# A two-layer decoder step on one core: low parts of the first output weights on VectorE, another projection order for two head pairs, and other ranks and slacks for the woven work

## The chip, the core and the metric

The kernel runs on one core of one Trainium2 chip. The metric is the device time of one execution in microseconds (us). In the profile the engines are PE (TensorE; PEld is its weight load), DVE (VectorE), ACT (ScalarE), POOL (GpSimd) and SP (SyncE, whose queue issues nearly all DMAs here).

## The reference

One inference step of a decoder with two layers, on a prompt of 1024 tokens and on 8 samples of 4 tokens (32 rows). Each layer computes `x + gate · Branch(RMSNorm(x)(1 + scale) + shift)`, with shift, scale and gate from a condition vector. The first branch is attention with a window of 128, 16 query heads and 4 key/value heads of 64. The second is gated DeltaNet with 16 value heads of 128, here taken as 8 pairs of heads that share a key head, in chunks of tokens. Cut to what matters:

```python
def swa_branch(h, w_in, sinks, w_out, k_buf=None, v_buf=None):
    q, k, v, z = jnp.split(h @ w_in, [...], axis=-1)
    attn = swa_prompt_core(q, k, v, sinks)            # samples: cached keys and values before them
    out = (attn * jax.nn.silu(z)) @ w_out

def gdn_branch(h, conv_buf, s0, w_in, conv_w, ...):
    xqkv, z, a, b = jnp.split(h @ w_in, [...], axis=-1)
    q, k, v = jnp.split(silu(conv(xqkv)), [...], axis=-1)   # q, k normalized
    # per chunk: a triangular system is solved (w_v, w_k), then in turn
    u = w_v_c - w_k_c @ S
    o = q_dec_c @ S + qk_c @ u
    S = S * g_tot_c + k_dec_c.T @ u
    out = (rms_norm(o, o_norm_g) * silu(z)) @ w_out
```

Outputs are both groups' final rows, the new key and value caches, the new convolution tails and the new DeltaNet states (8 samples × 16 heads × 128 × 128 and the prompt's). Everything is float32.

## The kernel before

**Products.** A large product is made as three TensorE products of split operands. Each operand is held as a high part (a rounded copy, made on ACT, as in `wh<-wr`) and a low part (raw minus high, a subtraction on DVE or POOL, as in `wl<-wr,wh`), and the products are high·high, high·low and low·high. The small products of the recurrence stay fp32. So TensorE's stream changes often between split products of 288, 384 or 512 columns and short fp32 products.

**Stages in time.** Attention runs to about 360 us (its opening, to about 70 us, is written out by hand), the samples' attention over cached keys from 360 to 388, the first layer's output projection from 394 to about 520, the eight DeltaNet pairs from 520 to 1353, and the closing from there: the second output projection, the samples' states and the final norm.

**What sets the order.** From the end of the opening on, the program's order is set by a planner inside the kernel. The stream of projection products is the backbone (`project`). Everything else is a job, a generator that yields a condition, issues some instructions and yields the next. `weave(gen, name, hq)` puts a job into the list by rank: `KT[name]` in the closing, `KR[hq][name]` for the jobs of one head pair, `K[name]` otherwise; a smaller rank comes first. After every projection product `stages()` goes through the list in that order and lets each job run as long as its condition holds. A condition can count products or columns passed (`later`, `pos[0] >= ...`), or compare times of a cost model that `Core.issued` keeps for each engine: `ready` wants the operands finished at TensorE's present time, `sure(by, ...)` with a margin, `soon` and `idle` with a slack (`AM`, and `AT` in the closing, in tenths of a us). The engines then run their streams in the order issued, and wait where an operand is late.

**Names and lines that follow.** L318 `SP` holds how many ticks after a projection's start its successor's two halves of weights are split (`ahead` in `projected`, L656 to L672). L1425 `load_wo` loads the first layer's output weights in sixteen pieces of 128x512 through four buffers, with three loads under way, each piece through

```python
                nc.scalar.copy(hi, raw)
                eng = "gpsimd" if hf else "vector"
                yield idle(eng, hi)
                getattr(nc, eng).tensor_sub(lo, raw, f(hi))
                placed.add((j, hf))
                fetch()
```

`ORD` (L2384) holds the order of the projections q, z, k and v of each pair; k belongs to the next pair. `chain` is the recurrence of a pair, eight steps in sequence: `S,kT` (TensorE), `vo` (DVE), `vo,UZ` (TensorE, into `ps_ob`), `uo` (ACT), `uo,ks` (TensorE), the new `S` (DVE); `S,qT` and `uo,DP` are the step's outputs. `vT`, `zl`, `Xd` and `UZ` are operands that ACT, DVE and POOL make for the pairs (`vT` and `zl` are turned on TensorE afterwards, into `ps_tr`). `modG,selt` spreads the gate rows over the partitions for the closing. `olo` and `ohi` are parts of the gated heads for the second output projection, `S1w` the samples' new states.

Of the kernel before, what the change touches and what calls it, by code (L numbers as in the profile page):

```python
# [18 lines left out]
NB = TP // P  # L19
# [278 lines left out]
def body(tc, I, O, cst_ap, dbg=None):  # L298
# [16 lines left out]

    nkeep = COFF["wmask"][0]
    ZB, VB, SB = 2, 3, 6
    SP = (1, 20)  # L318
    AM = (3, 12)
    AT = (-5, 5)  # L320
    EX = (2.2, 2.5, 0.8, 0.7)
    ES, EN, EL, EM = EX
    K = {'split': 13, 'add': 6, 'attend': 26, 'turning': 2, 'modulate': 27, 'cached': 16, 'wo': 48, 'turn': 0, 'ahead': 2, 'taps': 2, 'gating': 5, 'decay': 24, 'samples': 38, 'load': 6, 'mod': 1, 'shape': 9, 'decays': 23, 'prepare': 0, 'gather': 17, 'finish': 32, 'states': 28, 'core': 33, 'new': 11}
    KT = {'prepare': 3, 'gather': 35, 'finish': 63, 'states': 10, 'core': 7, 'new': 18, 'load': 27, 'gating': 6, 'samples': 6, 'output': 20}
    KR = [{'chain': 1, 'output': 3, 'solve': 5, 'invert': 21, 'blocks': 35, 'decayed': 22}, {'chain': 30, 'output': 2, 'solve': 19, 'invert': 31, 'blocks': 39, 'decayed': 37}, {'chain': 9, 'output': 2, 'solve': 29, 'invert': 19, 'blocks': 5, 'decayed': 11}, {'chain': 23, 'output': 23, 'solve': 4, 'invert': 4, 'blocks': 7, 'decayed': 17}, {'chain': 13, 'output': 11, 'solve': 12, 'invert': 7, 'blocks': 29, 'decayed': 27}, {'chain': 9, 'output': 15, 'solve': 6, 'invert': 16, 'blocks': 49, 'decayed': 27}, {'chain': 0, 'output': 1, 'solve': 11, 'invert': 20, 'blocks': 29, 'decayed': 14}, {'chain': 10, 'output': 2, 'solve': 33, 'invert': 28, 'blocks': 1, 'decayed': 53}]
    TB = (3, 0)
    SW = (20, 7)
    MS = (34, 13)
    AH, AI = (a / 10 for a in AM)
    ORD = ['zzkv', 'zqzvk', 'qzzkv', 'qzzvk', 'qzzkv', 'qvzzk', 'qzzkv', 'qvzz']  # L330
    MM = (8, 12)
    ORDER = [("q", 2), ("q", 3), ("q", 4), ("q", 5), ("z", 0), ("k", 1), ("z", 1), ("z", 2), ("q", 6), ("q", 7),
             ("z", 3), ("z", 4), ("z", 5), ("z", 6), ("z", 7)]
    SE = ("vector", "vector", "vector", "vector")
# [675 lines left out]
    if True:  # L1010
# [414 lines left out]
        def load_wo(j0):  # L1425

            pieces = [(j, hf) for j in range(j0, j0 + 4) for hf in range(2)]
            raws_ = []
            if j0:
                yield over("ahead")  # L1430

            def fetch():
                if pieces:
                    j, hf = pieces.pop(0)
                    pr, g = j // 4, j % 4
                    raw = (wp.tile([P, 512], F32, tag="wr", name="wr", bufs=4) if j0 else
                           sa.tile([P, 512], F32, tag="wor", name="wor", bufs=4))
                    for a in range(2):
                        hd = (2 * pr + a) * 4 + g
                        nc.sync.dma_start(raw[64 * a:64 * a + 64], wo_rows[hd * 64:hd * 64 + 64, hf * 512:(hf + 1) * 512])  # L1440
                    raws_.append((j, hf, raw))

            for _ in range(3):
                fetch()
            while raws_:
                j, hf, raw = raws_.pop(0)
                cs = slice(hf * 512, (hf + 1) * 512)
                hi, lo = whi[j][:, cs], wlo[j][:, cs]
                yield idle("scalar", raw)
                nc.scalar.copy(hi, raw)  # L1450
                eng = "gpsimd" if hf else "vector"
                yield idle(eng, hi)
                getattr(nc, eng).tensor_sub(lo, raw, f(hi))
                placed.add((j, hf))
                fetch()
# [5 lines left out]
        load, step, end = modulation_gate(0, at, 8, "wg")  # L1461
# [86 lines left out]
    if True:  # L1548
# [24 lines left out]
        def add_out(pj, i, t, hf):  # L1573

            parts = P if t < NB else TS
            ns = slice(hf * 512, (hf + 1) * 512)
            yield lambda: gathered[0] == 2 * i + hf and i in rows_
            xt = rows_[i][0:parts]
            if t < NB:
                yield idle("vector", pj)  # L1580
                y = x2.tile([P, 512], F32, tag="y", name="y", bufs=2)
                nc.vector.tensor_tensor(y, pj, gate[:, ns], ALU.mult)
                opened.pop(0)
            else:
# [12 lines left out]
                give("lg", pg)  # L1597
            eng = "vector" if i == NB and hf else "gpsimd"
            yield idle(eng, y, xt)
            getattr(nc, eng).tensor_tensor(xt[:, ns], xt[:, ns], y[0:parts], ALU.add)  # L1600
            if hf == 0:
                rows_["ss", i] = sm.tile([P, 2], F32, tag="ss", name="ss")[0:parts]
            yield soon(xt)
            nc.scalar.activation(y[0:parts], xt[:, ns], AF.Square, accum_out=rows_["ss", i][:, hf:hf + 1])
            gathered[0] += 1
            if hf == 1:
                nc.sync.dma_start(x1d[t * P:t * P + parts], xt)
                weave(shape(i, t, xt, rows_["ss", i], parts), "shape")
                if t == NB:
                    weave(modulation_gate(1, wp, 4, "wr"), "mod")  # L1610
# [272 lines left out]
    if True:  # L1883
# [446 lines left out]
        def load_out(*cuts):  # L2330
# [14 lines left out]
            while raws_:  # L2345
                hf, k, ns, raw = raws_.pop(0)
                yield lambda: whs[k] is not None
                yield sure(EL, raw)
                hi, lo = whs[k][:, ns], wls[k][:, ns]
                yield idle("scalar", raw)  # L2350
                nc.scalar.copy(hi, raw)
                eng = "gpsimd" if k % 2 else "vector"
                yield idle(eng, hi)
                getattr(nc, eng).tensor_sub(lo, raw, f(hi))
                loaded.add((k, hf))
                fetch()
# [60 lines left out]
        def prepare(b, part, t):  # L2417
# [5 lines left out]
            for kk in range(2):  # L2423
# [16 lines left out]
                olo = x3.tile([P, 4, P], F32R, tag="olo", name="olo", bufs=2)  # L2440
                yield idle("scalar", of)
                nc.scalar.copy(ohi, of)
                eng = "gpsimd" if kk else "vector"
                yield idle(eng, ohi)
                getattr(nc, eng).tensor_sub(olo, of, f(ohi))
                ohl.append((ohi, olo))
# [47 lines left out]
        def gather(pj, n, part, t, hf):  # L2494
# [541 lines left out]
```

## Time and profile before

| | |
|---|---|
| runs | 1619.73, 1619.86, 1620.67 us; median 1619.86 |
| profiled execution | 1618.79 us, span 1617.0 us |
| mean granted clock of TensorE | 0.997 |
| TensorE busy | 1581.2 us of the span |
| VectorE, ScalarE, GpSimd busy | 1204.8, 843.0, 222.7 us |
| DMA | 195.7 MB, mean 121 GB/s |

The three runs differ by 0.94 us. The profile is one further execution; its time lies 1.07 us under the median, and its span leaves out 1.8 us around the program. A busy TensorE is a modelled figure, since matmuls overlap: what it loses is better read from the starts of neighbouring products, and from the rows of waits, which give for a group of products the total idle time ahead of them, how often, and the longest.

### The profile page before, as it was taken

What the parts mean: (1) busy time and instruction counts of PE and PEld (TensorE: products, weight loads), DVE (VectorE), ACT (ScalarE), POOL (GpSimd) and SP (SyncE); (2) the same over time, 40 slices, a digit from 0 to 9 for tenths busy, and PEclk for the clock granted to TensorE, in tenths of its full rate; (3) what the DMA queues carried; (4) which work ended last, traced back from release to release, by engine and by line L of the source; (5) the groups of instructions that cost most, each with busy time, mean ns of one, the idle gap of its engine ahead of it and who ended that gap; (6) DMA issues with size and microseconds to landing.
All of it is one profiled execution on the core that took longest, in us unless ns stands there. A gap on an engine that the chain in (4) does not pass through costs nothing.

```text
span 1617.0 us, 30791 instructions
## 1 busy us (share of the span) xinstructions
PE 1581.2 (98%) x10714; PEld 1403.0 (87%) x10714; DVE 1204.8 (75%) x3773; ACT 843.0 (52%) x2422; POOL 222.7 (14%) x292
## 2 busy tenths in 40 slices
PE   9999999999999999999999999999999999999997
PEld 6888888988678999989999999998999997757776
DVE  5737677565665678987988769897679877858776
ACT  4635555444344655576465655665456564523332
POOL 1300000002223002020020000202002013233332
PEclk9999999999999999999999999999999999999999
DMA  9442220116343333233423324414243146685874
GB/s 363 154 140 79 79 81 28 40 51 148 105 146 108 106 84 80 81 90 80 133 53 95 99 57 113 99 49 120 61 126 76 45 104 195 207 270 169 298 264 165
DMA packets 178828, 195.72 MB, mean 121 GB/s; under 512 B 76848, under 2 KB 120720, under 8 KB 178640
## 3 DMA queue, kind: packets, MB, share of 16 engines
q1 hardware_dynamic: 178672, 193.75, 40.2%
q8 instruction: 85, 1.39, 0.4%
q14 instruction: 71, 0.58, 0.1%
HBM read 146.45 MB, written 49.27 MB: 121 GB/s over the span
## 4 chain that ended last, share of the span: by engine, by line
PE 77%; DVE 7%; DMA 5%; issue 4%; ACT 4%; POOL 2%; SPq 1%; POOLq 0%; DVEq 0%; ACTq 0%
PE ps_pj L84 45%; PE ps_mi L84 12%; PE ps_lg L84 9%; PE ps_ob L84 5%; PE ps_tr L84 4%; DMA zo<-in_xT 1%; ACT jc L84 1%; PE ps_pj L1480 1%; POOL xt L84 1%; SPq L84 1%; DVE vT L84 1%; DMA out_new_s_s<-S 1%; DVE hlo L84 1%; DVE fu L84 1%; PE ps_tr L1480 1%
## 5 line engine op out<-in xcount | busy, mean ns | idle before, releaser
L84 PE MATMUL ps_pj<-h2lo,wh 128*128 128x384 f32 (+1 forms) x1128 | 377.4, 335 | 0.0
L84 PE MATMUL ps_pj<-h2hi,wh 128*128 128x384 f32 (+1 forms) x1128 | 377.4, 335 | 0.0
L84 PE MATMUL ps_pj<-h2hi,wl 128*128 128x384 f32 (+1 forms) x1128 | 375.8, 333 | 1.2 <-DVE wl L84 1.2
L84 PEld LDWEIGHTS ps_pj<-h2hi,wl 128*128 128x128 f32 x1128 | 212.7, 189 | 3.7 <-DVE wl L84 1.5
L84 PEld LDWEIGHTS ps_pj<-h2lo,wh 128*128 128x128 f32 x1128 | 212.9, 189 | 2.3
L84 PEld LDWEIGHTS ps_pj<-h2hi,wh 128*128 128x128 f32 x1128 | 212.7, 189 | 2.3
L84 POOL TENSOR_TENSOR Xd<-Xc,cst 32x128 f32<-32x128 f32 x128 | 67.0, 524 | 436.8 <-DMA Xc<-Xdd 347.7
L84 PE MATMUL ps_pj<-hhi,wh 128*128 128x384 f32 (+1 forms) x376 | 123.9, 332 | 0.5 <-ACT hhi L84 0.4
L84 PE MATMUL ps_pj<-hlo,wh 128*128 128x384 f32 (+1 forms) x376 | 123.5, 331 | 0.1
L84 PE MATMUL ps_pj<-hhi,wl 128*128 128x384 f32 (+1 forms) x376 | 122.1, 328 | 0.0
L84 DVE TENSOR_TENSOR wl<-wr,wh 128x512 fp32r<-128x512 f32 x120 | 84.2, 703 | 19.4 <-ACT wh L84 18.6
L84 DVE SCALAR_TENSOR_TENSOR vT<-XR,cT,vT 128x384 f32<-128x384 f32 (+1 forms) x144 | 83.5, 588 | 11.8 <-ACT vT L84 10.5
L84 POOL TENSOR_TENSOR xt<-xt,y 128x512 f32<-128x512 f32 (+1 forms) x47 | 65.7, 1400 | 164.7 <-DVE y L84 137.6
L84 ACT CAST wh<-wr 128x512 fp32r<-128x512 f32 x128 | 78.5, 615 | 14.3 <-PE ps_pj L84 13.4
L84 PEld LDWEIGHTS ps_pj<-hlo,wh 128*128 128x128 f32 x376 | 70.6, 188 | 10.6 <-issue 9.8
L84 PEld LDWEIGHTS ps_pj<-hhi,wh 128*128 128x128 f32 x376 | 70.5, 188 | 6.7 <-issue 4.6
L84 ACT COPY XR<-ps_pj 128x384 f32<-128x384 f32 (+1 forms) x96 | 43.3, 451 | 60.1 <-PE ps_pj L84 60.0
L84 PEld LDWEIGHTS ps_pj<-hhi,wl 128*128 128x128 f32 x376 | 70.6, 188 | 3.7 <-issue 3.7
L84 ACT ACTIVATE qe<-ps_mi,Eg 128x128 f32<-128x128 f32 x112 | 35.0, 363 | 67.5 <-PE ps_mi L84 61.1
L84 DVE TENSOR_TENSOR X<-X,tmp 128x126 f32<-128x126 f32 (+22 forms) x248 | 63.8, 257 | 8.5
L84 ACT ACTIVATE prob<-prob,nm 128x256 f32<-128x256 f32 (+1 forms) x128 | 62.4, 491 | 14.1 <-DVE nm L84 13.8
L84 DVE TENSOR_TENSOR tmp<-X 128x126 f32<-128x126 f32 (+22 forms) x248 | 62.4, 252 | 6.2 <-POOL X L84 1.9
(557 smaller groups left out, 3866.1 us busy)
## 6 DMA issues: line engine op xcount, KB each, us to landing
wr<-in_gwb SPq DMA_DIRECT2D x96, 256.0 KB
S<-in_states SPq DMA_DIRECT2D x42, 256.0 KB
wm<-in_wm SPq DMA_DIRECT2D x16, 512.0 KB
wr<-in_winb SPq DMA_DIRECT2D x32, 256.0 KB
wmod<-in_w_mod SPq DMA_DIRECT2D x32, 256.0 KB
wm<-in_w_mod SPq DMA_DIRECT2D x32, 256.0 KB
DP<-gcr SPq DMA_DIRECT2D x64, 128.0 KB
zl<-zd SPq DMA_DIRECT2D x32, 256.0 KB
```

Of the source, the lines that this page charges most:

```text
L84: inst = fn(*args, **kwargs)
L1480: mm = nc.tensor.matmul(pv, x[:, k, t * P:t * P + parts], y[:, k % 2, :], start=(n == 0), stop=(n == 23))
```

## The change

The low parts of the first layer's output weights are all made on DVE (`GP[0]` is 0; eight subtractions of 128x512 leave POOL). The other entries of `GP` are 1 and leave their lines as they were. Pair 2 projects in the order z, q, z, k, v instead of q, z, z, k, v, and pair 5 in the order v, q, z, z, k instead of q, v, z, z, k. All ranks are drawn anew, most of them with other values. The split of the next weights may start after two ticks instead of one (`SP`), the slack of `idle` in the closing is 0.3 us instead of 0.5 (`AT`), the margin for the samples' states 1.7 us instead of 2.2 (`EX`), and three schedules by position have other starts and strides (`SW`, `MS`, `MM`).

```diff
-    SP = (1, 20)
+    SP = (2, 20)
     AM = (3, 12)
-    AT = (-5, 5)
-    EX = (2.2, 2.5, 0.8, 0.7)
+    AT = (-5, 3)
+    EX = (1.7, 2.5, 0.8, 0.7)
...
-    KT = {'prepare': 3, 'gather': 35, 'finish': 63, 'states': 10, 'core': 7, 'new': 18, 'load': 27, 'gating': 6, 'samples': 6, 'output': 20}
+    KT = {'prepare': 3, 'gather': 33, 'finish': 24, 'states': 19, 'core': 7, 'new': 14, 'load': 19, 'gating': 6, 'samples': 5, 'output': 23}
...
-    SW = (20, 7)
-    MS = (34, 13)
+    SW = (35, 1)
+    MS = (39, 13)
     AH, AI = (a / 10 for a in AM)
-    ORD = ['zzkv', 'zqzvk', 'qzzkv', 'qzzvk', 'qzzkv', 'qvzzk', 'qzzkv', 'qvzz']
-    MM = (8, 12)
+    GP = (0, 1, 1, 1, 1)
+    ORD = ['zzkv', 'zqzvk', 'zqzkv', 'qzzvk', 'qzzkv', 'vqzzk', 'qzzkv', 'qvzz']
+    MM = (7, 12)
...
-                eng = "gpsimd" if hf else "vector"
+                eng = "gpsimd" if hf and GP[0] else "vector"
```

TensorE has 9,020 matmuls before and after, DVE 3,775 and 3,783 instructions, POOL 297 and 289. The order of the products differs from about 100 us on. Three places in the two orders:

At the start of the first pair, on DVE, around 557 us. `DP` are decay blocks; `gss` and the `rsw`, `rst` behind it are the sixteen operations that make the norms of the keys; `wl` are low parts of the next projection's weights. The piece of the difference:

```order
 L84 COPY gbs<-g 128x16
 L84 COPY gbs<-bt 128x16
-L84 SCALAR_TENSOR_TENSOR DP<-DP,gc,cst 128x128 x5
+L84 SCALAR_TENSOR_TENSOR DP<-DP,gc,cst 128x128 x6
+L84 TENSOR_TENSOR wl<-wr,wh 128x512
 L84 TENSOR_SCALAR gss<-gss 128x8
 L84 TENSOR_SCALAR rsw<-gss 128x8
```

and after the sixteen operations:

```order
 L84 TENSOR_TENSOR sj<-beta,rk 128x16
 L84 TENSOR_TENSOR sd<-sj,Kd 128x16
-L84 TENSOR_TENSOR wl<-wr,wh 128x512 x2
-L84 SCALAR_TENSOR_TENSOR DP<-DP,gc,cst 128x128 x11
-L84 SCALAR_TENSOR_TENSOR UZ<-ps_mi,sj,DP 128x128 x16
+L84 TENSOR_TENSOR wl<-wr,wh 128x512
+L84 SCALAR_TENSOR_TENSOR DP<-DP,gc,cst 128x128 x10
+L84 SCALAR_TENSOR_TENSOR UZ<-ps_mi,sj,DP 128x128 x13
```

One of the two subtractions `wl` has moved from behind the sixteen small operations to ahead of them; the other has stayed.

At the end of the pair stage, on TensorE, from the last projection products on (`ps_pj<-h2hi,wl` is the last of them, `ps_pj<-h2hi,ohi` the first of the second output projection). Before:

```order
L84 MATMUL ps_ob<-vo,UZ 128x128 x2
L84 MATMUL ps_pj<-h2hi,wl 128x288
L84 MATMUL ps_mi<-uo,ks 128x128 x2
L84 MATMUL ps_mi<-S,qT 128x256
L84 MATMUL ps_mi<-uo,DP 128x128 x2
L84 MATMUL ps_mi<-S,kT 128x256
L84 MATMUL ps_ob<-vo,UZ 128x128 x2
L84 MATMUL ps_mi<-uo,ks 128x128 x2
L84 MATMUL ps_lg<-modG,selt 128x512
L84 MATMUL ps_mi<-S,qT 128x256
L84 MATMUL ps_mi<-uo,DP 128x128 x2
L84 MATMUL ps_pj<-h2hi,ohi 128x512
```

and now:

```order
L84 MATMUL ps_pj<-h2hi,wl 128x288
L84 MATMUL ps_mi<-uo,ks 128x128 x2
L84 MATMUL ps_mi<-S,qT 128x256
L84 MATMUL ps_mi<-uo,DP 128x128 x2
L84 MATMUL ps_mi<-S,kT 128x256
L84 MATMUL ps_ob<-vo,UZ 128x128 x2
L84 MATMUL ps_mi<-uo,ks 128x128 x2
L84 MATMUL ps_mi<-S,qT 128x256
L84 MATMUL ps_mi<-uo,DP 128x128 x2
L84 MATMUL ps_lg<-modG,selt 128x512
L84 MATMUL ps_mi<-S,kT 128x256
L84 MATMUL ps_lg<-modG,selt 128x512
```

Behind the last of these rows `ps_pj<-h2hi,ohi` follows at once. The stretch between the two projections holds the same kinds of products; one `S,kT` and a second `modG,selt` have come into it, and the chain, which had five steps left behind the last projection product, has six.

At the very end, on DVE, behind the last but one product with the gate. Before:

```order
L84 SCALAR_TENSOR_TENSOR xt<-xt,rs,fng 128x512 x2
L84 SCALAR_TENSOR_TENSOR S1w<-S1w,gtb,ps_mi 128x128 x4
L84 TENSOR_TENSOR y<-ps_tr,gp 128x512
L84 TENSOR_TENSOR xt<-xt,y 128x512
L84 TENSOR_TENSOR y<-ps_ob,gp 128x512
L84 TENSOR_TENSOR xt<-xt,y 128x512
L84 TENSOR_TENSOR sv<-ss 128x1
```

and now:

```order
L84 TENSOR_TENSOR y<-ps_tr,gp 128x512
L84 SCALAR_TENSOR_TENSOR xt<-xt,rs,fng 128x512
L84 SCALAR_TENSOR_TENSOR S1w<-S1w,gtb,ps_mi 128x128 x8
L84 SCALAR_TENSOR_TENSOR xt<-xt,rs,fng 128x512
L84 TENSOR_TENSOR xt<-xt,y 128x512
L84 TENSOR_TENSOR y<-ps_ob,gp 128x512
L84 TENSOR_TENSOR xt<-xt,y 128x512
L84 SCALAR_TENSOR_TENSOR S1w<-S1w,gtb,ps_mi 128x128 x4
L84 TENSOR_TENSOR sv<-ss 128x1
```

Eight updates `S1w` stand ahead of the last additions, where four stood, and four more between the last addition and `sv`, the sum of squares of the final norm.

More of the change, by code (lines that the diff above doesn't have):

```diff
@@ L317, in body @@
     ZB, VB, SB = 2, 3, 6
-    SP = (1, 20)
+    SP = (2, 20)
     AM = (3, 12)
-    AT = (-5, 5)
-    EX = (2.2, 2.5, 0.8, 0.7)
+    AT = (-5, 3)
+    EX = (1.7, 2.5, 0.8, 0.7)
     ES, EN, EL, EM = EX
-    K = {'split': 13, 'add': 6, 'attend': 26, 'turning': 2, 'modulate': 27, 'cached': 16, 'wo': 48, 'turn': 0, 'ahead': 2, 'taps': 2, 'gating': 5, 'decay': 24, 'samples': 38, 'load': 6, 'mod': 1, 'shape': 9, 'decays': 23, 'prepare': 0, 'gather': 17, 'finish': 32, 'states': 28, 'core': 33, 'new': 11}
@@ L324, in body @@
-    KT = {'prepare': 3, 'gather': 35, 'finish': 63, 'states': 10, 'core': 7, 'new': 18, 'load': 27, 'gating': 6, 'samples': 6, 'output': 20}
-    KR = [{'chain': 1, 'output': 3, 'solve': 5, 'invert': 21, 'blocks': 35, 'decayed': 22}, {'chain': 30, 'output': 2, 'solve': 19, 'invert': 31, 'blocks': 39, 'decayed': 37}, {'chain': 9, 'output': 2, 'solve': 29, 'invert': 19, 'blocks': 5, 'decayed': 11}, {'chain': 23, 'output': 23, 'solve': 4, 'invert': 4, 'blocks': 7, 'decayed': 17}, {'chain': 13, 'output': 11, 'solve': 12, 'invert': 7, 'blocks': 29, 'decayed': 27}, {'chain': 9, 'output': 15, 'solve': 6, 'invert': 16, 'blocks': 49, 'decayed': 27}, {'chain': 0, 'output': 1, 'solve': 11, 'invert': 20, 'blocks': 29, 'decayed': 14}, {'chain': 10, 'output': 2, 'solve': 33, 'invert': 28, 'blocks': 1, 'decayed': 53}]
+    K = {'split': 13, 'add': 0, 'attend': 40, 'turning': 0, 'modulate': 17, 'cached': 16, 'wo': 37, 'turn': 0, 'ahead': 2, 'taps': 2, 'gating': 5, 'decay': 23, 'samples': 38, 'load': 6, 'mod': 3, 'shape': 12, 'decays': 58, 'prepare': 58, 'gather': 8, 'finish': 10, 'states': 28, 'core': 2, 'new': 4}
@@ new lines, in body @@
+    KT = {'prepare': 3, 'gather': 33, 'finish': 24, 'states': 19, 'core': 7, 'new': 14, 'load': 19, 'gating': 6, 'samples': 5, 'output': 23}
+    KR = [{'chain': 4, 'output': 15, 'solve': 5, 'invert': 18, 'blocks': 40, 'decayed': 22}, {'chain': 31, 'output': 31, 'solve': 12, 'invert': 31, 'blocks': 39, 'decayed': 37}, {'chain': 9, 'output': 2, 'solve': 29, 'invert': 41, 'blocks': 1, 'decayed': 11}, {'chain': 23, 'output': 23, 'solve': 4, 'invert': 4, 'blocks': 0, 'decayed': 23}, {'chain': 10, 'output': 2, 'solve': 45, 'invert': 40, 'blocks': 1, 'decayed': 56}, {'chain': 8, 'output': 15, 'solve': 6, 'invert': 16, 'blocks': 49, 'decayed': 12}, {'chain': 0, 'output': 1, 'solve': 11, 'invert': 20, 'blocks': 34, 'decayed': 14}, {'chain': 10, 'output': 2, 'solve': 45, 'invert': 28, 'blocks': 1, 'decayed': 56}]
@@ L1597, in add_out @@
                 give("lg", pg)
-            eng = "vector" if i == NB and hf else "gpsimd"
+            eng = "gpsimd" if GP[3] and not (i == NB and hf) else "vector"
             yield idle(eng, y, xt)
@@ L2351, in load_out @@
                 nc.scalar.copy(hi, raw)
-                eng = "gpsimd" if k % 2 else "vector"
+                eng = "gpsimd" if k % 2 and GP[1] else "vector"
                 yield idle(eng, hi)
@@ L2442, in prepare @@
                 nc.scalar.copy(ohi, of)
-                eng = "gpsimd" if kk else "vector"
+                eng = "gpsimd" if kk and GP[2] else "vector"
                 yield idle(eng, ohi)
@@ L2502, in gather @@
             opened.pop(0)
-            eng = "vector" if n >= 2 * LB else "gpsimd"
+            eng = "gpsimd" if GP[4] and n < 2 * LB else "vector"
             yield idle(eng, y)
```

## The prediction

> **What bounds the kernel now.** I read four views in this order: the page (busy time and the chain of work that ended last), the busy time of three stages, what TensorE waited for in each stage, and then the single rows of the largest waits.
>
> ```profile
> PE 1581.2 (98%) x10714; PEld 1403.0 (87%) x10714; DVE 1204.8 (75%) x3773; ACT 843.0 (52%) x2422; POOL 222.7 (14%) x292
> PE 77%; DVE 7%; DMA 5%; issue 4%; ACT 4%; POOL 2%; SPq 1%; POOLq 0%; DVEq 0%; ACTq 0%
> 520.00:1350.00 830.00, 821.69 (x6008) 787.86 (x6005) 679.03 (x2149) 487.04 (x1440) 74.25 (x157) 1.00 0.33 88
> 1350.00:1400.00 50.00, 46.36 (x240) 37.15 (x239) 39.36 (x101) 25.48 (x72) 15.63 (x18) 0.97 0.71 212
> 1400.00:1610.00 210.00, 201.59 (x990) 149.06 (x988) 151.36 (x412) 73.86 (x170) 70.69 (x52) 1.00 0.72 237
> ```
>
> In a stage row, the length is followed by busy PE, weight loads, DVE, ACT and POOL. TensorE is the bound; DVE is busy for 1204.8 us of 1617 and the chain spends only 7% on it. The change keeps all TensorE products (9,020 matmuls in both orders), so it can act only through TensorE's idle time and through the seams between kinds of products. Idle is 8.3 us of the pair stage (830 − 821.69), 3.6 at its end (50 − 46.36) and 8.4 in the closing (210 − 201.59). Of the pair stage's idle time the waits show:
>
> ```profile
> PE ps_tr L84 <- ACT vT L84: 2.5, 5, 0.9
> PE ps_lg L84 <- POOL Xd L84: 1.7, 2, 1.4
> PE ps_tr L84 <- DVE zl L84: 1.3, 4, 0.4
> PE ps_pj L84 <- DVE wl L84: 1.2, 1, 1.2
> PE ps_lg L84 <- DVE UZ L84: 0.4, 1, 0.4
> ```
>
> These are total, times and longest. No engine is short here; each is one product issued a little before its operand exists. What counts for such a wait is how much other TensorE work stands between the product that starts the chain to the operand and the product that needs it. That distance is what ranks and slacks move, and it can be counted in both orders.
>
> **Seams (T1).** The orders have three changes between fp32 and split products fewer, and 42 → 34 direct returns from 32-row products to projections.
>
> ```profile
> 706.56 0.29 PE L84 MATMUL ps_pj<-h2lo,wh 128*128 128x288 f32 x1
> 706.78 0.74 PE L84 MATMUL ps_lg<-UZ,M 128*32 128x64 f32 x16
> 707.45 0.40 PE L84 MATMUL ps_pj<-h2hi,wl 128*128 128x288 f32 x1
> 707.69 0.30 PE L84 MATMUL ps_pj<-h2hi,wh 128*128 128x288 f32 x1
> 707.82 0.60 PE L84 MATMUL ps_tr<-erl,vo 128*128 128x128 f32 x4
> ```
>
> Projections of 288 columns stand 0.13 us apart (707.69 to 707.82). Entering the 32-row block takes 0.22 (706.56 to 706.78) and coming back 0.24 (707.45 to 707.69): 0.2 us a visit. Eight returns less, at 0.1 each: −0.8 us. If the block is only entered from another fp32 block, the seam is moved and not saved: 0. With the entries saved too it is −1.6. I take −0.8, since the counts show the returns.
>
> **The pair stage (T2).** The largest wait is this one.
>
> ```profile
> 557.82 0.17 DVE L84 TENSOR_SCALAR gss<-gss 128x8 f32<-128x8 f32 x1
> 560.87 0.18 DVE L84 TENSOR_TENSOR sd<-sj,Kd 128x16 f32<-128x16 f32 x1
> 560.96 1.28 DVE L84 TENSOR_TENSOR wl<-wr,wh 128x512 fp32r<-128x512 f32 x2
> 560.21 0.34 PE L84 MATMUL ps_pj<-h2lo,wh 128*128 128x384 f32 x1
> 561.70 0.44 PE L84 MATMUL ps_pj<-h2hi,wl 128*128 128x384 f32 x1 [1.15 <-DVE wl L84]
> ```
>
> Sixteen small operations (557.82 to 560.87) stand on DVE ahead of the two subtractions that make the low parts. From 560.21 to 561.70 is 1.49 us where neighbours stand 0.17 apart: 1.32 lost. In the new order the first subtraction stands ahead of the sixteen: it ends near 558.5 (557.8 + 1.28 / 2), three microseconds before its reader wants it, −1.3. The second ends at 562.24 as before, since the same operations stand ahead of it; its reader, twelve products on (12 × 0.173 = 2.1 us), now comes at 562.5. That is just in time: I charge nothing, and 0.3 if the cover of these twelve is gone.
>
> ```profile
> 1113.47 1.13 PE L84 MATMUL ps_lg<-Xd,UZ 128*128 128x96 f32 x8 [1.44 <-POOL Xd L84]
> 597.24 0.55 PE L84 MATMUL ps_tr<-erl,vT 128*128 128x128 f32 x3 [0.93 <-ACT vT L84]
> 1253.01 0.55 PE L84 MATMUL ps_tr<-erl,vT 128*128 128x128 f32 x3 [0.25 <-ACT vT L84]
> ```
>
> All four waits on zl (1.3 us) and the one on UZ (0.4) get more TensorE work between start and use than they lacked: −1.7. By start to start a wait costs some 0.15 more than its idle column says (wl: 1.32 against 1.15): −0.8 for these five. The Xd at 1113.47 gets three or four projections of 0.13 us more, the vT at 597.24 two of 0.17: −0.5 and −0.4, with the rest of both left. The vT at 1253.01 loses two: +0.2. With wl that is −4.5. Against it stand four places where the new order has less cover than such an operand needed in this trace: a zl, an Xd, a vT and a UZ. At the mean of the rows above (0.3, 0.85, 0.5, 0.4) all four cost 2.1; I charge half, +1.0, as an operand's lateness varies by as much as it lacks there. T2 = −3.5. Bounds: −5 if the four cost nothing and half of the unlisted idle goes too (8.3 less the 7.1 of the five rows is 1.2), 0 if as much returns elsewhere.
>
> **The first layer's output weights (T3).** Eight subtractions move from POOL to DVE.
>
> ```profile
> L84 POOL TENSOR_TENSOR wlo<-wor,whi x4: 1262/1283/1296, 368.4 to 383.2; 128x512 fp32r<-128x512 f32 x4
> L84 DVE TENSOR_TENSOR wlo<-wor,whi x4: 679/690/1781, 369.8 to 382.4; 128x512 fp32r<-128x512 f32 x4
> PE ps_mi L84 <- ACT whi L84: 0.7, 1, 0.7
> PE ps_lg L84 <- DMA KT<-in_keysT: 1.6, 2, 0.9
> ```
>
> POOL loses 8 × 1.28 = 10.2 us and DVE gains 8 × 0.69 = 5.5 us over some 40 us in which TensorE stays the bound. The reader of the last low part came after whi, which was awaited, so the faster subtraction alone buys nothing. But a weight's buffer comes free, and the next load is issued on SP's queue, 0.6 us earlier (1.28 − 0.69) where DVE is free at once: up to −0.6 at the wait on whi. The other way, SP's loads of cached keys are queued behind these weight loads, and a subtraction that DVE takes one operation (0.69) late holds them: +0.7 at the waits on KT. I take 0, bounds −0.6 and +0.9. DVE's longest here took 1781 ns, while POOL ran the other one; its median is 690. The Trainium skill ("SBUF — State Buffer", section "SBUF: two separate sides") says that DVE and GpSimd share one port pair, which one of them holds alone for a whole instruction. The trace agrees by 1781 against 690; by that rule the move also gives DVE back about 1.1 us, which no TensorE wait of this stage asks for.
>
> **The end of the pair stage (T4).** Here the chain of the last pair outlives the projections.
>
> ```profile
> 1353.45 0.38 PE L84 MATMUL ps_pj<-h2hi,wl 128*128 128x288 f32 x1
> 1354.21 0.71 PE L84 MATMUL ps_mi<-uo,ks 128*128 128x128 f32 x4 [0.38 <-ACT uo L84]
> 1356.97 0.67 PE L84 MATMUL ps_mi<-S,kT 128*128 128x256 f32 x2 [1.16 <-DVE S L84]
> 1358.08 0.75 PE L84 MATMUL ps_ob<-vo,UZ 128*128 128x128 f32 x4 [0.45 <-DVE vo L84]
> 1359.36 1.22 PE L84 MATMUL ps_mi<-uo,ks 128*128 128x128 f32 x4 [0.53 <-ACT uo L84]
> PE ps_mi L84 <- DVE S L84: 2.3, 2, 1.2
> 1355.00:1360.00 5.00, 2.86 (x15) 2.08 (x14) 3.29 (x8) 2.53 (x6) 1.92 (x2) 0.94 0.95 322
> 1360.00:1365.00 5.00, 5.00 (x17) 3.28 (x17) 3.12 (x9) 1.62 (x4) 0.38 (x1) 0.72 0.86 269
> ```
>
> One step of the chain with nothing beside it idles 1.16 + 0.45 + 0.53 = 2.1 us, and after it the granted clock (the figure after the busy times) falls to 0.94 and 0.72: 5 × 0.06 + 5 × 0.28 = 1.7 us more. In the new order six steps are left after the last projection, where five were. The first of them is as bare as before; the next has the gate rows' products (modG) and three products of the output projection at a time (512 columns, 0.23 us each by the 0.173 of 384) between its links. With that cover its links should idle little of their 2.1: I charge +0.3, bounds −1.1 (the second wait on S, 2.3 less 1.16, gets more work ahead of it) and +2.1 + 1.7 = +3.8. The Trainium skill ("TensorE: Matmul & The Clock Gate", Part 1) puts the lowered clock down to an idle window of about 3.4 us, and the return to as long a busy one. The rows agree in kind (0.72 follows a stretch with 2.86 of 5 us busy). By the page a second window at half rate would cost 1.7 us (an estimate: half of 3.4), as the rows have it.
>
> **The closing and the tail (T5, T6).**
>
> ```profile
> PE ps_pj L84 <- POOL olo L84: 1.7, 2, 1.0
> PE ps_pj L84 <- DVE ohi L84: 1.1, 1, 1.1
> PE ps_pj L84 <- DVE olo L84: 0.3, 1, 0.3
> 1605.82 1.12 DVE L84 SCALAR_TENSOR_TENSOR S1w<-S1w,gtb,ps_mi 128x128 f32<-128x128 f32 x4 [0.25 <-PE ps_mi L84]
> 1610.45 0.29 DVE L84 TENSOR_TENSOR sv<-ss 128x1 f32<-128x1 f32 x1 [0.85 <-ACT sq L84]
> ```
>
> In the new order the olo of DVE and the second of POOL get several products more ahead of their readers (−0.3 and −0.7); the other olo and ohi keep their places. The new places for vo, ohi and kb together may cost as much as they save: I take T5 = −0.3, bounds −1.5 and +2. At the very end the last updates of the samples' states (S1w, 1.12 us on DVE) stand between the last addition and sv, and eight more stand ahead of the last product with the gate. The 0.85 us in which DVE waits for the squares hides most of one; I take T6 = +0.7, bounds 0.3 (1.12 − 0.85) and 1.5.
>
> **Sum.** −0.8 − 3.5 + 0 + 0.3 − 0.3 + 0.7 = −3.6 us. The profiled execution took 1618.8 us with a span of 1617.0; minus 3.6 it would be 1615.2. It lies 1.1 under the median of the runs, so on that scale: 1619.9 − 3.6 = **1616.3 us**.
>
> **The rivals.**
> - *Covers are only exchanged.* Every microsecond of work that stands ahead of one operand is taken from another's. For it: in the closing, ohi and one olo keep their waits word for word; against it: wl and all of zl gain at once, and the moved subtraction has no victim in sight. Then T2 and T5 are 0: −0.8 + 0.3 + 0.7 = +0.2, 1620.1 us.
> - *Slower: the bare chain.* The point that decides is the second step after the last projection (the place of 1356.97 to 1359.36 of before, one step on). If modG and the output products come before its links and not between them, because their own operands are late or the links are ready only afterwards, the step idles 2.1 us and brings a second window at low clock, 1.7. With T2 eaten up by new waits it is −0.8 + 3.8 + 0.7 = +3.7: 1623.6 us. For it: six steps instead of five; against it: three products between links in the order.
> - *Only the low parts count.* If the new ranks change the order at places where nothing waits, T3 alone is left: 1619.3 to 1620.8. The order speaks against it: wl and zl, which are awaited, do move.
>
> **How the numbers follow.** A measurement of this kernel tells about 0.2% (3.2 us) from no change. The forecast has 0.5, the exchange 0.28, the bare chain 0.16, the low parts alone 0.06. The forecast lies only 0.4 us past the bound of 3.2; yet its cases reach further down than up, since five of the six terms have room below. So I give faster 0.5, same 0.34, slower 0.16. The range: down, T1 −1.6, T2 −5, T3 −0.6, T4 −1.1, T5 −1.5 and T6 +0.3 make −9.5, so I go to 1610; up, it ends at 1622.5, which holds part of the bare chain.
>
> **What would show it.** T1: fewer 32-row blocks next to projections, with their 0.24 us. T2: no wait on wl, those on zl near 0, Xd's longest under 1.1; wrong if the stage's idle stays above 7 us. T3: waits on KT and whi within 0.9 of before. T4: one bare stretch with a clock of about 0.7 and not two. T6: sv about 0.7 later after the last product. The prediction falls if the idle of the pair stage is unchanged, or if the closing idles over 10 us.

## The result and the profile after

The changed kernel takes 1615.92 us (median of 17 runs) beside 1621.18 us for the kernel before (17 runs): ratio 0.9967, 95% interval 0.9956 to 0.9978. That is 5.3 us less (3.6 to 7.1). Its profiled execution has a span of 1614.5 us against 1617.0, only 2.5 us less, since the execution of before that was profiled was one of its quicker ones (1618.8 us, where its 17 runs have a median of 1621.2).

Stages are best compared between products that both orders have. From the timeline of each trace I took the start of the first DeltaNet projection, of the last projection product of 288 columns, of the first product of the second output projection, and of TensorE's last product, and then the end of the span:

| us | to the first DeltaNet projection | pair stage | its end | closing | tail | span |
|---|---|---|---|---|---|---|
| before | 508.3 | 845.2 | 9.7 | 244.3 | 9.5 | 1617.0 |
| changed | 508.0 | 839.9 | 9.0 | 246.1 | 11.5 | 1614.5 |

The pair stage gives 5.3 us, and 3.8 come back: 1.8 in the closing and 2.0 behind TensorE's last product. Part of the pair stage's gain is only moved work. Twelve products, 3.1 us of TensorE's work by the medians of their kinds, have left the stage. Eight of them (one more step of the chain, 2.2 us) now stand behind the last projection: with the `modG` that changes places, 1.3 us of work more in the stage's end and 0.9 more in the closing. The other four (`dg,xt`, 0.9 us) now stand ahead of the first DeltaNet projection. What is left of the pair stage's gain, 2.2 us, is waiting.

The busy time of the same three stages in the changed kernel (length, then busy PE, weight loads, DVE, ACT, POOL, then the granted clock):

```profile
520.00:1350.00 830.00, 822.21 (x6023) 789.54 (x6021) 677.71 (x2154) 488.49 (x1445) 74.39 (x158) 1.00 0.34 89
1350.00:1400.00 50.00, 45.10 (x237) 34.93 (x236) 39.48 (x100) 25.62 (x79) 15.75 (x19) 1.00 0.62 199
1400.00:1610.00 210.00, 198.72 (x970) 148.93 (x969) 154.18 (x417) 73.11 (x161) 68.45 (x51) 0.99 0.71 236
```

and the waits of TensorE in its pair stage (520 to 1350 us; total, times, longest):

```profile
PE ps_tr L84 <- ACT vT L84: 4.2, 7, 0.9
PE ps_lg L84 <- DVE UZ L84: 2.1, 2, 1.5
PE ps_ob L84 <- DVE UZ L84: 0.7, 1, 0.7
PE ps_lg L84 <- ACT th L84: 0.4, 1, 0.4
PE ps_tr L84 <- DVE zl L84: 0.3, 1, 0.3
```

The waits on wl (1.2) and Xd (1.7) are gone, and of the four on zl one is left. But vT went from 2.5 to 4.2 and UZ from 0.4 to 2.8. The listed waits add up to 7.7 us, where all of those before (the five rows shown and two of 0.4 and 0.3) made 7.8. By this view alone the covers were exchanged. It leaves out what a wait costs beyond its idle column, and all the short ones. By start to start (each product's distance to the next less the median of its kind and seam) the stage's lateness is 30.4 us against 33.2; how the seams are sorted moves that difference by about a microsecond. Grouped by the product that waits, Xd gave 2.4, wl 1.3 and zl 1.2, and vT and UZ took 2.7.

The cure of wl looks as foreseen. DVE's timeline of the changed kernel:

```profile
557.98 0.68 DVE L84 TENSOR_TENSOR wl<-wr,wh 128x512 fp32r<-128x512 f32 x1
558.58 0.16 DVE L84 TENSOR_SCALAR gss<-gss 128x8 f32<-128x8 f32 x1
561.60 0.17 DVE L84 TENSOR_TENSOR sd<-sj,Kd 128x16 f32<-128x16 f32 x1
561.71 0.69 DVE L84 TENSOR_TENSOR wl<-wr,wh 128x512 fp32r<-128x512 f32 x1
```

The first subtraction ends at 558.7, ahead of the sixteen small operations, and the second at 562.4, as before. TensorE has no wait on either.

At the end of the pair stage, TensorE's rows and the granted clock in the changed kernel:

```profile
1347.90 0.29 PE L84 MATMUL ps_pj<-h2hi,wl 128*128 128x288 f32 x1
1350.66 0.75 PE L84 MATMUL ps_ob<-vo,UZ 128*128 128x128 f32 x4 [0.45 <-DVE vo L84]
1352.46 0.71 PE L84 MATMUL ps_mi<-uo,ks 128*128 128x128 f32 x4 [1.05 <-ACT uo L84]
1356.94 0.49 PE L84 MATMUL ps_pj<-h2hi,ohi 128*128 128x512 f32 x1 [0.73 <-ACT ohi L84]
1350.00:1355.00 5.00, 3.50 (x20) 2.54 (x19) 3.89 (x9) 2.84 (x8) 2.88 (x2) 1.00 0.75 186
1355.00:1360.00 5.00, 4.03 (x19) 2.49 (x18) 1.57 (x5) 1.96 (x4) 0.00 (x0) 1.00 1.03 399
```

The bare step idles 0.45 + 1.05 = 1.5 us. The next one is covered by modG, and the output projection then waits for its own operand (0.73). The clock stayed at 1.00 here. In the tail DVE has, with TensorE's last products ahead of it:

```profile
1602.69 0.40 PE L84 MATMUL ps_ob<-h2lo,ohi 128*128 128x512 f32 x1
1602.89 1.12 DVE L84 SCALAR_TENSOR_TENSOR S1w<-S1w,gtb,ps_mi 128x128 f32<-128x128 f32 x4 [0.28 <-PE ps_mi L84]
1603.93 0.75 DVE L84 SCALAR_TENSOR_TENSOR xt<-xt,rs,fng 128x512 f32<-128x512 f32 x1
1604.60 0.69 DVE L84 TENSOR_TENSOR xt<-xt,y 128x512 f32<-128x512 f32 x1
1605.20 0.69 DVE L84 TENSOR_TENSOR y<-ps_ob,gp 128x512 f32<-128x512 f32 x1
1606.53 1.12 DVE L84 SCALAR_TENSOR_TENSOR S1w<-S1w,gtb,ps_mi 128x128 f32<-128x128 f32 x4
1607.56 0.19 DVE L84 TENSOR_TENSOR sv<-ss 128x1 f32<-128x1 f32 x1
```

The last product with the gate, `y`, starts 2.1 us after the product that it needs has ended (1603.1), because four updates of the states, a scaling of a row and an addition stand ahead of it in DVE's order. In the kernel before it started 0.3 us after its product (1608.19, with TensorE's last product at 1607.46 to 1607.85).

### The profile page after: what moved, and what is told of

The parts are those of the page before. It is cut to its first block, busy times and chain, and to the rows that moved or that the text cites. A ratio compares the mean times of both kernels' runs of the same rounds, so it can differ in the third digit from the quotient of the medians.

```text
span 1614.5 us, 30776 instructions
## 1 busy us (share of the span) xinstructions
PE 1579.1 (98%) x10714; PEld 1404.6 (87%) x10714; DVE 1203.3 (75%) x3781; ACT 843.1 (52%) x2422; POOL 209.9 (13%) x284
## 5 line engine op out<-in xcount | busy, mean ns | idle before, releaser
L84 ACT ACTIVATE prob<-prob,nm 128x256 f32<-128x256 f32 (+1 forms) x128 | 62.3, 489 | 15.5 <-DVE nm L84 15.4
```

Of the source, the lines that this page charges most:

```text
L84: inst = fn(*args, **kwargs)
```

## The experiments

Three theories stood against each other. **A**: the gain is cover in the pair stage, and the parts of the change add up. **B**: every new order is a new draw; covers are exchanged, and no part has a value of its own. **C**: the low parts on DVE are what counts. The names in the expectations: before, changed and so on are as above; each kernel was timed beside the kernel before on the same chip, and none beside the changed kernel, so that two ratios are compared through their intervals. All twelve are in this table, with the stages as above:

| kernel | ratio (95%) | to first DeltaNet projection | pair stage | its end | closing | tail |
|---|---|---|---|---|---|---|
| low parts only | 0.9987 (0.9976–0.9997) | 506.6 | 846.2 | 8.1 | 245.5 | 9.9 |
| SP only | 0.9992 (0.9980–1.0004) | 513.0 | 842.4 | 9.6 | 245.8 | 9.6 |
| pair ranks and orders only | 1.0047 (1.0033–1.0061) | 512.4 | 852.5 | 9.5 | 243.3 | 9.5 |
| MS only | 1.0029 (1.0019–1.0040) | 508.7 | 850.6 | 9.9 | 243.5 | 9.6 |
| K, KR, ORD, SP, MM | 0.9989 (0.9980–0.9997) | 508.3 | 843.9 | 8.0 | 247.0 | 9.6 |
| closing's numbers and MS | 1.0058 (1.0046–1.0070) | 508.2 | 847.8 | 12.7 | 248.4 | 10.9 |
| closing's numbers | 1.0036 (1.0023–1.0049) | 509.9 | 844.8 | 12.6 | 247.8 | 10.9 |
| changed, low parts shared | 0.9980 (0.9969–0.9991) | 510.0 | 842.7 | 8.0 | 246.8 | 11.1 |
| changed, closing's numbers and MS of before | 0.9979 (0.9968–0.9989) | 506.3 | 842.4 | 9.7 | 247.0 | 10.0 |
| changed, MS of before | 0.9977 (0.9967–0.9987) | 509.0 | 842.9 | 7.9 | 245.4 | 11.4 |
| changed, KT, AT, EX of before | 0.9966 (0.9954–0.9978) | 508.3 | 840.8 | 8.1 | 248.5 | 10.0 |
| changed, additions on DVE | 1.0053 (1.0039–1.0067) | 507.4 | 842.0 | 9.2 | 261.5 | 10.7 |

### The low parts alone, and the change without them

```diff
-                eng = "gpsimd" if hf else "vector"
+                eng = "vector"
```

> The kernel before with one line changed: all low parts of the first layer's output weights on DVE. The order of TensorE's products differs from before in 10 places only. Theory A (the gain is TensorE's cover in the pair stage, the low parts buy nothing): ratio 1.000, within 0.0006 (1 us) of it; waits on KT and whi together within 0.9 us of the 2.3 before. Theory C (the low parts matter, through POOL's and DVE's shared time or earlier weight loads): ratio 0.998 or less.

Measured 0.9987, 2 us, from a change in ten places of TensorE's order. The only wait over 0.2 us left in this stage (360 to 520 us) is

```profile
PE ps_lg L84 <- DMA KT<-in_keysT: 1.2, 1, 1.2
```

so those on whi (0.7), vc (0.4) and sp (0.3) are gone, and KT fell from 1.6: 1.8 us of idle. The time to the first DeltaNet projection fell by 1.7 us (508.3 to 506.6), although this execution lost 1.7 us to a lowered clock at 10 to 15 us (5 × (1 − 0.66)). The subtractions of this kernel, by tile (least, median, longest in ns):

```profile
L84 DVE TENSOR_TENSOR wlo<-wor,whi x8: 668/678/686, 369.7 to 384.5; 128x512 fp32r<-128x512 f32 x8
L84 DVE TENSOR_TENSOR wlo<-wr,whi x8: 682/684/694, 389.3 to 398.9; 128x512 fp32r<-128x512 f32 x8
```

The last ends at 399.6, where the kernel before starts its last at 405.5. SP's issues come forward with them: the last of these loads is issued by 395.7 us here and by 400.7 before. Behind this stage the order is that of before. Its pair stage, 846.2 against 845.2, has 1.7 us of a lowered clock in it (530 to 540 us).

The other side, the changed kernel with `GP = (1, 1, 1, 1, 1)`:

> The changed kernel with the low parts shared between DVE and POOL again (15 places of TensorE's order differ from the changed kernel, in the first layer's end and a few behind it). If the low parts are worth the same here as alone (0.9987 of the kernel before; by their profile 1.7 us of waits up to 508 us): ratio 0.998 (0.997 to 0.999), waits on whi, vc and sp back. If they gain only in the old order: 0.9967, as with them.

0.9980 with, as put down, 2.0 us more up to the first DeltaNet projection (510.0 against 508.0). 0.9980 and 0.9967 have intervals that overlap, so the 0.13% in the new order is not shown by these times alone. All fourteen profiles together say more. With the time lost to a lowered clock (5 × (1 − clock), summed over stretches of 5 us) taken out, the six with all low parts on DVE need 504.9 to 508.0 us up to the first DeltaNet projection (mean 506.5), and the eight others 508.0 to 509.2 (mean 508.4); three kernels of each group have the four products `dg,xt` (0.9 us) in it besides. So the low parts are worth some 2 us whatever the order behind them: a part that does have a value of its own. Theory C holds for 2 of the 5 us and no more.

### The split of the next weights alone

```diff
-    SP = (1, 20)
+    SP = (2, 20)
```

> The kernel before with only the split of the next weights allowed after two ticks and not one. In the order one subtraction wl stands ahead of the sixteen small operations again, and 409 places of TensorE's order differ, so nearly the whole pair stage is reordered by this one number; the tail is that of before; six chain steps are left behind the last projection. Theory A: the wait of 1.15 us on wl is gone and the stage from the first layer's end to the last projection is 1 to 4 us shorter; ratio 0.9975 to 0.9995. Theory B (all covers are exchanged; a new order is a new draw): the wl wait is gone too, but as much returns at other rows: ratio between 0.999 and 1.002.

0.9992, not to be told from no change; the pair stage is 2.8 us shorter, but 2.2 of that is the chain step that now stands behind the last projection. Xd is no longer among the waits (1.7 us before) and zl has 0.4 instead of 1.3, so this number does change covers; UZ has 1.7 instead of 0.4. But the wait on wl is not gone, it is 1.9 us: the subtraction that I had seen ahead of `gss` stands nine rows ahead of it, and one stands there, ten rows ahead, in the order of before too; both halves that TensorE wants next still come behind the sixteen operations (at 566.0 and 567.1, `gss` at 562.9). My reading of that order was wrong. It was not this number that cured wl.

### MS alone, and the change without it

```diff
-    MS = (34, 13)
+    MS = (39, 13)
```

> The kernel before with only MS, the projection positions at which the second layer's gate products run, five later. 93 places of TensorE's order differ, and one subtraction wl stands ahead of the sixteen small operations as in the changed kernel, while ranks, SP and projection orders are those of before. Theory M (this number, not SP or the ranks, takes the wait on wl away): no wait on wl near 560 us, the stage up to the last projection 1.3 us shorter, ratio 0.999 (0.998 to 1.0). If the wl wait only moves on, as with the closing's numbers together (2.1 us at a later wl): 1.000 to 1.002.

The wait near 560 us is gone, so this number moves that subtraction. But the kernel is slower, 1.0029: the pair stage takes 850.6 us (3.4 of it at a lowered clock). Its timeline shows what came instead:

```profile
729.41 0.71 PE L84 MATMUL ps_mi<-uo,ks 128*128 128x128 f32 x4 [1.63 <-ACT uo L84]
818.05 0.44 PE L84 MATMUL ps_pj<-h2hi,wl 128*128 128x384 f32 x1 [2.00 <-DVE wl L84]
```

One wl is cured, another comes 256 us later. The other side, the changed kernel with `MS = (34, 13)`:

> The changed kernel with MS of before. In the order both subtractions wl stand where they stood before, and the order of the pair stage differs from the changed kernel in 63 places. Theory M: the wait of 1 to 2 us on wl is back near 560 us, ratio 0.9975 (0.9967 to 0.9985). If the wait on wl is paid for elsewhere: 0.9967.

0.9977, and the wait is back (1.40 us at 563.6, and 0.9 at 789.9). This agrees with theory M as to the place. The other traces bear it out: all eight kernels with `MS = (34, 13)` have the wait between 559 and 567 us (1.0 to 1.9 us), and none of the six with `MS = (39, 13)`. What the place is worth is another matter: the intervals of 0.9977 and 0.9967 overlap, so its worth, some 0.1%, is not shown.

### The pair ranks and projection orders alone

```diff
-    KR = [{'chain': 1, 'output': 3, 'solve': 5, 'invert': 21, 'blocks': 35, 'decayed': 22}, ...]
+    KR = [{'chain': 4, 'output': 15, 'solve': 5, 'invert': 18, 'blocks': 40, 'decayed': 22}, ...]
...
-    ORD = ['zzkv', 'zqzvk', 'qzzkv', 'qzzvk', 'qzzkv', 'qvzzk', 'qzzkv', 'qvzz']
+    ORD = ['zzkv', 'zqzvk', 'zqzkv', 'qzzvk', 'qzzkv', 'vqzzk', 'qzzkv', 'qvzz']
```

> The kernel before with the ranks of the head pairs (KR) and the projection orders of pairs 2 and 5 alone. The first pair is as before, then 63 places of TensorE's order differ. Theory A (the pair stage gains by zl, UZ and Xd, which get more cover there): the stage is 1 to 2 us shorter, ratio 0.9985 to 0.9995. Theory B (exchange): 1.000 to 1.001, with fewer waits on zl and more on vT and UZ.

Slower by 0.47%: worse than either theory had it. The pair stage is 7.3 us longer, with the same work. Its waits there:

```profile
PE ps_tr L84 <- ACT vT L84: 6.4, 8, 1.7
PE ps_pj L84 <- DVE wl L84: 1.7, 2, 1.3
PE ps_ob L84 <- DVE UZ L84: 1.3, 1, 1.3
PE ps_tr L84 <- DVE zl L84: 1.0, 3, 0.4
```

Xd is cured here too (2.2 us by start to start before, 0.1 now), and vT pays for it, 2.5 to 6.4. These ranks belong to a stream that SP and the first layer's ranks have shifted; that this is why they fail alone is argued and not shown.

### All of the pair stage's numbers without the closing's

The kernel before with K, KR, ORD, SP and MM of the change.

> The kernel before with the ranks K and KR, the projection orders ORD, SP and MM of the changed kernel, and without the low parts and the closing's numbers. Six chain steps behind the last projection, the tail of before. Theory A: all of the pair stage's gain (5 us by the two profiles up to the last projection) without the 1.9 us that the tail costs: ratio 0.9955 to 0.997, not slower than the changed kernel. Theory B: between 0.998 and 1.001. Theory C: 1.000.

0.9989: faster than before, but a third of the change, not all of it. The pair stage is 1.3 us shorter than before (1.7 us of a lowered clock at 560 to 570 included), not 5, and 2.2 us of work has left it. The wait on wl is still there (1.81 us at 561.9), as MS is that of before. Since KR and ORD alone cost 0.47%, K, SP and MM together do more for them than SP did by itself (0.9992); K and MM were not run alone.

### The closing's numbers alone, with and without MS

```diff
-    AT = (-5, 5)
-    EX = (2.2, 2.5, 0.8, 0.7)
+    AT = (-5, 3)
+    EX = (1.7, 2.5, 0.8, 0.7)
...
-    KT = {'prepare': 3, 'gather': 35, 'finish': 63, 'states': 10, ...}
+    KT = {'prepare': 3, 'gather': 33, 'finish': 24, 'states': 19, ...}
...
-    SW = (20, 7)
-    MS = (34, 13)
+    SW = (35, 1)
+    MS = (39, 13)
```

> The kernel before with only the closing's ranks, slack, margin and schedules by position (KT, AT, EX, SW, MS) of the changed kernel. The pair stage keeps five chain steps behind the last projection, and the tail is that of the changed kernel (three pairs U,kb in the last ten rows of TensorE, S1w between the last addition and sv). Theory A: the time from TensorE's last product to the span's end is 11.4 us instead of 9.5, the closing itself is unchanged: ratio 1.001 (1.0005 to 1.002). If the closing's numbers are what gains: 0.998 or less.

Slower by 0.58%, where 0.1% was expected; only the tail (10.9, with 11.4 put down) is near it. MS, which I had counted with the closing, acts from the first layer's end on. The second kernel leaves it as it was:

> The kernel before with KT, AT, EX and SW of the changed kernel, without MS. TensorE's order is that of before up to the last projections, and the closing and the tail have the changed numbers. If the closing's own order is what cost 9 us with these numbers and MS together: ratio 1.004 to 1.006, long waits (K 3.7, ohi 2.1) and granted clocks below 0.8 behind 1355 us. If MS was: 1.001, by the tail's 1.5 us alone.

0.36% slower, with an order that is that of before up to the last projections. Of the nine microseconds that its span is longer, 2.9 lie at the pair stage's end, 3.5 in the closing and 1.4 in the tail; the rest lies ahead of that, where the order is the same and this execution lost 1.7 us to a lowered clock at 10 to 15 us. The timeline, DVE first:

```profile
1399.80 0.55 DVE L84 TENSOR_TENSOR vs<-kept,cT 128x384 f32<-128x384 f32 x1
1406.46 0.69 DVE L84 TENSOR_TENSOR vs<-vs,tp 128x512 f32<-128x512 f32 x1
1409.14 0.68 DVE L84 TENSOR_TENSOR K<-ps_lg,K 32x512 fp32r<-32x512 f32 x1
1409.88 0.75 PE L84 MATMUL ps_lg<-erl,vs 128*128 128x128 f32 x4 [3.72 <-DVE K L84]
```

The samples' convolution (vs) takes DVE from 1399.8 to 1407.1, the keys K come behind it, and TensorE waits 3.7 us. In the changed kernel the last of these (`vs<-vs,tp`) runs at 1390.45 and K at 1395.27, and no product waits on K. And a long wait is paid twice. The same kernel, with the granted clock behind the busy times:

```profile
1355.00:1360.00 5.00, 2.40 (x14) 1.74 (x13) 3.47 (x9) 2.95 (x7) 2.75 (x3) 1.00 0.92 299
1360.00:1365.00 5.00, 4.48 (x15) 3.69 (x16) 1.71 (x6) 1.30 (x4) 0.76 (x1) 0.50 0.91 320
1410.00:1415.00 5.00, 3.66 (x25) 1.87 (x25) 2.33 (x5) 3.22 (x9) 1.27 (x1) 0.62 0.71 240
1415.00:1420.00 5.00, 5.00 (x31) 3.22 (x27) 1.79 (x11) 0.59 (x1) 0.00 (x0) 0.70 0.92 253
```

Summed over the stretches of 5 us from 1355 us on, 5 × (1 − clock) is 8.5 us here and 1.7 in the kernel before. The difference, 6.8, is most of the 7.8 us lost there, as far as TensorE had work in these stretches.

### The change without the closing's numbers

KT, AT, EX, SW and MS of before in the changed kernel, which is also the low parts and the pair stage's numbers together.

> The changed kernel with the closing's ranks, slack, margin and schedules (KT, AT, EX, SW, MS) of the kernel before, so low parts and pair stage of the change alone. Parts add up: low parts alone 0.9987 and pair stage alone 0.9989 make 0.9976 (0.9965 to 0.9987); the tail is that of before (9.5 us behind TensorE's last product). By the parts the closing's numbers, 1.0058 alone, must then be a gain of 0.001 in the new order. If the closing's numbers hurt here as they do alone: 0.992 or less.

0.9979: the parts that were 0.9987 and 0.9989 alone do add up (0.9976). Their intervals allow the sum and don't prove it. So the closing's numbers and MS, 1.0058 alone, are 0.9967 / 0.9979 = 0.9988 here, a small gain or nothing. Why K comes in time there is seen (the convolution stands earlier), which of the numbers places it so is not.

### The change with the tail of before

KT, AT and EX of before in the changed kernel.

> The changed kernel with KT, AT and EX of before, but its own SW and MS: TensorE's and DVE's order is that of the changed kernel up to the closing (66 places differ, behind the last projection), and the last U,kb stands eleven rows before TensorE's last product as before. Theory A: the tail from TensorE's last product to the end is 9.5 us instead of 11.5, the rest as in the changed kernel: 0.9955 (0.9945 to 0.9965), faster than both kernels. Theory B (what the tail saves returns in the closing): 0.9967 (0.996 to 0.9985).

0.9966. The tail is 10.0 instead of 11.5 as meant, and the closing takes 248.5 instead of 246.1, with K awaited again (1.1 us) and kb for 1.9. The ratio lies inside both ranges and does not decide; by this one profile theory B holds for the closing.

### The closing's additions on DVE

```diff
-    GP = (0, 1, 1, 1, 1)
+    GP = (0, 1, 1, 1, 0)
```

> The changed kernel with the closing's additions to the rows (xt<-xt,y, 128x512) on DVE instead of POOL. The last U,kb then stands 36 rows before TensorE's last product. POOL takes 1.4 us for an addition and DVE some 0.7, in a closing in which DVE is busy for 154 of 210 us. If the additions' length is what the output rows wait for, the closing and tail are 1 to 3 us shorter: 0.995 to 0.996. If DVE becomes the later engine there, the waits on ohi, y and S grow: 0.998 to 1.001.

The closing becomes 15.4 us longer. TensorE's waits in it and the clock behind them:

```profile
PE ps_lg L84 <- DVE oH L84: 4.7, 1, 4.7
PE ps_tr L84 <- DVE y L84: 3.0, 1, 3.0
1480.00:1485.00 5.00, 1.52 (x6) 1.25 (x6) 3.98 (x18) 1.08 (x2) 0.12 (x1) 0.51 0.26 87
1485.00:1490.00 5.00, 2.67 (x7) 2.25 (x8) 3.69 (x10) 1.25 (x4) 0.00 (x0) 0.50 0.75 246
```

The two waits differ. oH is no later than in the changed kernel: DVE finishes it at 1482.65 us in both. What changed is TensorE's order: in the changed kernel 22 products of the output projection (1477.9 to 1482.9) stand ahead of the product that needs oH, and here they stand behind it. The wait on y is DVE's own: updates of the states, a low part and one of the moved additions (1485.99) stand ahead of it (1486.59). Where the low parts were moved DVE was busy for 27 of 50 us (360 to 410 us), in the closing for 154 of 210; that this load is what makes the one move gain and the other lose is argued and not shown.

No kernel beat the changed one beyond its interval.

## Why the prediction was right, point by point

The time (1616.3 against 1615.9, 3.6 us less forecast and 5.3 measured, interval 3.6 to 7.1) came out of terms of which half were off, with errors of opposite sign; that the sum came so near is in part luck. With moved work and the time at a lowered clock (1.7 us in each, at 1355 to 1365 before and at 1470 to 1475 after) taken out, the two profiles differ like this:

| us | forecast | the two profiles |
|---|---|---|
| up to the first DeltaNet projection (T3) | 0 | −1.2 |
| pair stage (T1 and T2) | −4.3 | −2.2 |
| its end (T4) | +0.3 | −0.3 |
| closing (T5) | −0.3 | −0.8 |
| tail (T6) | +0.7 | +2.0 |
| sum | −3.6 | −2.5 |

The profiles show 2.5 of the 5.3 us; the rest lies between executions and is not placed.

- **Seams (T1, −0.8)** did not come. With each kind of seam at its median over both traces, they cost about the same, 42.4 us from 70 us on before and 42.1 after. The price of a visit held or was higher (0.09 in, 0.19 and 0.11 out), but the returns are moved: of the 48 blocks `UZ,M` of 32-row products, 37 were followed by a projection before and 29 are now, and those followed by another fp32 product went from 11 to 18, by a transpose from none to 1. That was the bound of 0.
- **Pair stage (T2, −3.5)** had its direction right and its size not. Three traces have the order of before in this stage (before, low parts only, closing's numbers) and three that of after (changed, KT, AT and EX of before, additions on DVE). With the 3.1 us of moved work added back and the lowered clock taken out the stage takes 844.5 to 845.2 us in the first three and 843.0 to 843.9 in the others: −1.4 by their means. wl, zl and Xd went as the covers said, and Xd gave 2.4 instead of 0.5. The step that failed is the charge for places with new too little cover: +1.0 was put down, and vT and UZ took 2.7. One UZ alone waited 1.5 us. A smaller slip stands in the working for wl: its reader was due at 560.4 us (561.70 less the 1.32 lost), so a subtraction that ends at 558.5 is two microseconds early and not three.
- **Low parts (T3, 0)** were worth 2 us. The chain named, an earlier buffer and so an earlier load on SP, is the one that the trace of the low parts alone shows, but "up to −0.6 at the wait on whi" counted one piece where sixteen follow each other; the last starts 6.6 us earlier (398.9 against 405.5). In the profile of the changed kernel itself the gain mostly hides: the last subtraction starts at 404.5, whi fell to 0.3, but sp and spT wait 0.8 and 0.9. On the port, the Trainium skill's rule ("SBUF — State Buffer", "SBUF: two separate sides") fits: with POOL out of this work none of DVE's sixteen subtractions is over 694 ns, where beside POOL's they took up to 1364 and 1781.
- **End of the pair stage (T4, +0.3)**: −0.7, with 1.3 us more work in it. One bare step, as forecast, and no second. Its idle is the same (0.38 + 1.16 + 0.45 + 0.53 = 2.5 before, 0.45 + 1.05 + 0.73 + 0.23 = 2.5 now); what differs is the clock, 1.7 us, and that is no property of the order: the kernel with the low parts alone has the rows of before here (waits of 0.38, 1.16, 0.45, 0.52) and ran them at 1.00. The slower rival, a bare chain that brings a second window at low clock, came true in another kernel: the closing's numbers alone have 12.6 us at this place, 3.4 of it lost to the lowered clock.
- **Closing (T5, −0.3)**: +1.8, of which 0.9 is moved work and 1.7 a lowered clock (0.66 at 1470 to 1475) that the kernel before had elsewhere; −0.8 is left.
- **Tail (T6, +0.7)**: +2.0 (+1.2 to +1.9 in the other kernels with the closing's numbers), outside its bounds of 0.3 and 1.5. The step that was wrong: I charged the S1w behind the last addition, and that one is hidden (sv comes 0.95 us after the additions, 0.85 before). The eight ahead of the last additions, which I only mentioned, are what counts: with a scaling and an addition they put the last `y` 2.1 us behind its product, where it was 0.3.

The rival "covers are only exchanged" was nearer to the truth than its 0.28: in the pair stage more than half of what Xd, wl and zl gave was taken back at vT and UZ, and SP, KR with ORD, MS and the numbers of the closing gained nothing that could be told by themselves. "Only the low parts count" holds for two fifths of the gain.

What stays open: why K, SP and MM turn ranks that cost 0.47% by themselves into part of a gain. The runs show the interaction, and its places (vT, UZ, wl); they don't show one cause.

## What to carry to other kernels

When TensorE is busy for 98% and its idle time is many small late operands, count for each the work between what starts it and what needs it, in the order before and after; but charge as much for places that lose cover as for those that gain: here they took 2.7 of 4.9 us. Before two profiles are compared stage by stage, take out the work that has moved from one stage to another and the time at a lowered clock. Numbers that were chosen together can't be judged one by one: here seven sets by themselves gave from 0.9987 to 1.0058, and all together 0.9967. Before work is moved to the faster engine, look at what else that engine has to do there, and at what then stands ahead of the last operations of the program.

## What the runs showed of the hardware

The granted clock falls after a stretch in which TensorE idles for about half, but not each time: the same rows at the end of the pair stage ran at 0.72 in one execution and at 1.00 in another. A fall costs about 1.7 us, or twice or three times that where it lasts longer (5 × (1 − clock), summed), and products of 512 columns then stand 0.43 us apart and not 0.23. In the changed kernel, just behind two waits in a row:

```profile
1469.20 0.50 PE L84 MATMUL ps_pj<-h2hi,ohi 128*128 128x512 f32 x1 [0.88 <-ACT ohi L84]
1470.69 0.50 PE L84 MATMUL ps_pj<-h2hi,olo 128*128 128x512 f32 x1 [0.99 <-POOL olo L84]
1471.54 0.63 PE L84 MATMUL ps_pj<-h2hi,olo 128*128 128x512 f32 x1
1471.97 0.63 PE L84 MATMUL ps_pj<-h2lo,ohi 128*128 128x512 f32 x1
```

The Trainium skill ("TensorE: Matmul & The Clock Gate", Part 1) describes a window that runs freely, whatever the kernel does, so that the same idle stretch may or may not fill one; the two executions agree with that. Idle time is not all of it: in five of the fourteen kernels the clock fell near 535 us, just behind a group of small transposes (`erl,abT`, 64x32), in a stretch in which the profile shows TensorE busy throughout; why is open. In the kernel with the low parts alone:

```profile
530.00:535.00 5.00, 5.00 (x33) 4.66 (x32) 1.93 (x6) 2.37 (x5) 0.00 (x0) 0.88 0.00 0
535.00:540.00 5.00, 5.00 (x29) 5.00 (x28) 4.42 (x12) 3.17 (x6) 0.00 (x0) 0.77 0.00 0
```

The lowered clock makes long waits dearer than their length: 8.5 us of lowered clock in the kernel with the closing's numbers, and 12 in that with the additions on DVE.

One execution of an unchanged order differs from the next by 1 to 2 us in the pair stage (845.2 and 846.2; 839.9, 840.8 and 842.0), and most of that is the lowered clock: without the 1.7 us that it took from 846.2 and from 842.0, they are 845.2 and 844.5, and 839.9, 840.8 and 840.3. So a stage of a single profile tells a microsecond only when its clock is looked at too.
